# Differential queries and keys in 32-feature groups, gathered by transfers inside SBUF

## The chip, the core and the metric

One core of one Trainium2 chip runs the whole program. The metric is the device time in microseconds, the median of several runs; a profiled execution gives the trace beside it. Engines are named as the profile names them: PE (matmul), PEld (its weight loads), DVE (VectorE), ACT (ScalarE), POOL (GpSimd), SP (the queue that issues nearly all transfers).

## What is computed

A layer with two kinds of heads on 512 frames of width 2048: retention on one half, differential attention on the other, then an output projection and a gated projection. The part that the change touches is this (h heads of 2 × 64 features; `dv` are the values):

```python
u = rmsnorm(h, attn_norm[i])
z = u @ w_in[i]
...
dq = rmsnorm(dq.reshape(b, s, DIFF_HEADS, 2, DIFF_DH), diff_qn[i])
dk = rmsnorm(dk.reshape(b, s, DIFF_HEADS, 2, DIFF_DH), diff_kn[i])
...
sc = jnp.einsum('bqhcd,bkhcd->bhcqk', q_blk, kf)
pr = jax.nn.softmax(jnp.where(mask, sc, -jnp.inf), axis=-1)
attn = pr[:, :, 0] - lam * pr[:, :, 1]
out = jnp.einsum('bhqk,bkhe->bqhe', attn, vf)
```

The mask is causal in chunks of 64 frames, so a block of 128 queries sees 128, 256, 384 or 512 keys. Each of the 16 head components (8 heads × 2) is normed over its 64 features.

## The kernel before

Every float32 product is made of three matmuls on a high and a low part (`split`, `mm3`, L134 to L146): high times high, high times low, low times high. Features stand on the partitions, the 512 frames along the free dimension.

**Projections.** A chunk is 256 columns of a weight matrix. `wchunk` (L149) loads four blocks of 128 rows (512 KB) into the tile `raw` with the tag `wraw`, of which there are two buffers, and splits them into `wh` (ACT, L137) and `wl` (DVE, L138), of which there are four each. `wide_chunk` (L163) does the same for 512 columns at once. `proj_fm` (L225) accumulates a chunk in two of the four PSUM banks with the tag `acc`, `proj_wide` (L245) in all four. A load waits until the splits have read the buffer that it overwrites; a split waits until PE is done with the `wh` and `wl` four places before. Transfers and splits are given a high priority (`AHEAD`), so they stand as early in their queues as buffers allow. Each engine's queue, SP's among them, runs strictly in its order.

**Order of the work.** `run` advances a projection generator; at each yield `tick` counts up and runs what `agenda` holds for that tick. A tick is 12 matmuls of 512 columns. A projection of 256 columns has 8 ticks, a wide one 16. `after(n, f)` puts f at n ticks from now. A scheduler then lays out each engine's queue.

**Differential heads** go in four pairs (`pair_jobs`, L529): chunk `dq`, chunk `dk`, then other projections (`dg`, the wide `dv`), beside which the pair's steps are done. Here a chunk's two accumulators hold one head each: partitions 0 to 63 the first component, 64 to 127 the second. `qk_done` (L536) multiplies each accumulator with the row norm R1 (L541, frees the bank), then for each of the two heads makes a sum of squares (`squares`, L320: square, high, low), two matmuls against the block matrix `bd` (L347, L349), a chain of Ln, Exp, Square and three DVE operations (`rsqrt`, `normed`), and `stack_q` or `stack_k`, which write the operands in halves of 64 partitions: `qa` holds high over low of a component's queries, `k0` its keys' high part twice, `kz` their low part over zeros. The two norms are due at ticks `QK` after the chunk. `scores` (L475) makes, for each component, two matmuls into a bank of the tag `sc` (two banks), masks (L486), takes the maximum (L487) and the exponential with its sum (L488). `turn` transposes the probabilities, `values` multiplies with the values, `norm` ends a head. Their ticks are `SCORES`, `TURNS` and `VALUES`, counted from the end of `dk`.

Of the kernel before, what the change touches and what calls it, by code (L numbers as in the profile page):

```python
# [12 lines left out]
F32 = mybir.dt.float32  # L13
# [25 lines left out]
def f(ap):  # L39
    return ap.bitcast(F32)  # L40
# [3 lines left out]
def tile_layer(  # L44
# [42 lines left out]
    ct = const.tile([P, 43], F32, name="ct")  # L87
# [36 lines left out]
    g_dk = ct[:, 41:42]  # L124
# [4 lines left out]
    g_dq = const.tile([P, 1], F32, name="g_dq")  # L129
    nc.vector.tensor_scalar(g_dq, ct[:, 40:41], 0.125, None, ALU.mult)  # L130
    g_sub = const.tile([P, 1], F32, name="g_sub")
    nc.vector.tensor_scalar(g_sub, ct[:, 42:43], 0.8, None, ALU.mult)
# [16 lines left out]
    def wchunk(wd, n0, nk, name):  # L149
        wv = wd.rearrange("(kb p) n -> p kb n", p=P)  # L150
        for k0 in range(0, nk, 4):
            kn = min(4, nk - k0)
            with tc.high_priority(offset=AHEAD):
                raw = wpool.tile([P, 4, CW], F32, tag="wraw", name=f"wr_{name}_{k0}", bufs=2)
                nc.sync.dma_start(raw[:, :kn, :], wv[:, k0:k0 + kn, n0:n0 + CW])
# [164 lines left out]
    def squares(src, eps, name, pool=tmp):  # L320
        sq = pool.tile([P, S], F32, tag="sq", name=f"sq_{name}", bufs=2)
        nc.scalar.activation(sq, src, AF.Square)
        sh = pool.tile([P, S], F32R, tag="hi", name=f"sqh_{name}", bufs=1)
        sl = pool.tile([P, S], F32R, tag="lo", name=f"sql_{name}", bufs=1)
        nc.scalar.activation(sh, sq, AF.Identity, bias=eps)
        nc.vector.scalar_tensor_tensor(sl, sq, eps, f(sh), ALU.add, ALU.subtract)
        return sq, sh, sl

    def squares2(src, eps2, name, pool):

        lo, hi = slice(0, 64), slice(64, P)
        sq = pool.tile([P, S], F32, tag="sq", name=f"sq_{name}", bufs=2)
# [8 lines left out]
        return sq, s2, None  # L341

    def normed(t, sq, sel, width, tag, name, cut=None):

        z, sh, sl = sq
        ss = bank(tag, 1, f"ss_{name}")
        nc.tensor.matmul(ss, lhsT=sel, rhs=sh, start=True, stop=sl is None)  # L347
        if sl is not None:
            nc.tensor.matmul(ss, lhsT=sel, rhs=sl, start=False, stop=True)  # L349
# [90 lines left out]
    with ExitStack() as st:  # L440
        dp = st.enter_context(tc.tile_pool(name="dp", bufs=2))

        kz = [[dp.tile([P, S], F32R, tag=f"kz{j}{i}", name=f"kz{j}{i}", bufs=1) for i in range(2)]
              for j in range(2)]
        for pair in kz:
            for i, oth in enumerate((A1, A0)):
                nc.vector.memset(f(pair[i])[oth], 0.0)

        def stack_q(t, h):
            qa = dp.tile([P, S], F32R, tag="qa", name=f"qa{h}")  # L450
            qb = dp.tile([P, S], F32R, tag="qb", name=f"qb{h}")
            nc.scalar.activation(qa[A0], t[A0], AF.Copy, scale=g_dq[A0])
            nc.scalar.activation(qb[A1], t[A1], AF.Copy, scale=g_dq[A1])
            nc.vector.scalar_tensor_tensor(qa[A1], t[A0], g_dq[A0], f(qa)[A0], ALU.mult, ALU.subtract)
            nc.vector.scalar_tensor_tensor(qb[A0], t[A1], g_dq[A1], f(qb)[A1], ALU.mult, ALU.subtract)
            return qa, qb

        def stack_k(t, h):
            k0 = dp.tile([P, S], F32R, tag="k0", name=f"k0{h}")
            k1 = dp.tile([P, S], F32R, tag="k1", name=f"k1{h}")  # L460
            z0, z1 = kz[h % 2]
            nc.scalar.activation(k0[A0], t[A0], AF.Copy, scale=g_dk[A0])
            nc.scalar.activation(k1[A1], t[A1], AF.Copy, scale=g_dk[A1])
            nc.vector.tensor_copy(k0[A1], f(k0)[A0])
            nc.vector.tensor_copy(k1[A0], f(k1)[A1])
            nc.vector.scalar_tensor_tensor(z0[A0], t[A0], g_dk[A0], f(k0)[A0], ALU.mult, ALU.subtract)
            nc.vector.scalar_tensor_tensor(z1[A1], t[A1], g_dk[A1], f(k1)[A1], ALU.mult, ALU.subtract)
            return k0, k1

        def diff_steps(h, pair):  # L470
# [4 lines left out]
            def scores(b):  # L475
                qa, qb = pair["q", j]
                k0, k1 = pair["k", j]
# [4 lines left out]
                for i, (qs, ks) in enumerate(((qa, k0), (qb, k1))):  # L482
# [28 lines left out]
            def values():  # L511
# [9 lines left out]
                own["sq"] = squares2(own["o"], eps_d, f"d{h}", dp)  # L521

            def norm():
                normed(own["o"], own["sq"], ones, P, ("tp", "o")[j], f"d{h}", cut=thr)
                nc.vector.scalar_tensor_tensor(on_d[h], own["o"], g_sub, on_d[h], ALU.mult, ALU.mult)
# [3 lines left out]
        def pair_jobs(hp):  # L529
            pair = {}  # L530

# [4 lines left out]
            def qk_done(which, stack):  # L536
# [76 lines left out]
    with ExitStack() as st:  # L613
# [20 lines left out]
        def ret_steps(h):  # L634
# [34 lines left out]
            def norm():  # L669
                normed(on_r[h], own["sq"], ones, P, "tp", f"r{h}")  # L670
# [254 lines left out]
```

## Time and profile before

| | |
|---|---|
| median of 3 runs | 1083.37 us (1083.04 to 1083.54) |
| the profiled execution's own time | 1083.01 us |
| its span, first to last instruction | 1081.2 us |
| PE busy | 1074.7 us, 99% |
| PE weight loads busy | 900.7 us, 83% |
| DVE busy | 652.9 us, 60% |
| ACT busy | 561.2 us, 52% |
| transfers | 111.15 MB, 103 GB/s over the span |

A matmul's own time in the trace (389 ns for 512 columns) runs from its start to the end of its pipeline, and the next one starts before it ends. What a matmul costs PE is therefore the distance between two starts. "Idle before" of a group is time in which the engine did nothing just before its instructions, with what ended the wait.

### The profile page before, as it was taken

Reading aid. Unit: us, or ns where it says so; the run is one execution under the profiler, and the core shown is the slowest. Engines: PE = TensorE matmul, PEld = TensorE weight load, DVE = VectorE, ACT = ScalarE, POOL = GpSimd, SP = SyncE. Lnnn points to the kernel's source line nnn. Section 1 sums busy time; section 2 is a strip of 40 time slices with the busy share of each in tenths; the row PEclk is TensorE's granted clock in tenths of the full one; section 3 lists DMA queues with packets and bytes.
Section 4 is the critical chain, followed back from the end, with each engine's and each line's share of the span. In section 5 each row is a group of like instructions: output and inputs, shape, how many; then the busy total and the mean of one; then the engine's idle time right before and its main releaser. Section 6 shows DMA issues by size and latency. Waiting matters only on the chain.

```text
span 1081.2 us, 13724 instructions
## 1 busy us (share of the span) xinstructions
PE 1074.7 (99%) x5090; PEld 900.7 (83%) x5090; DVE 652.9 (60%) x1211; ACT 561.2 (52%) x1044; POOL 4.9 (0%) x14
## 2 busy tenths in 40 slices
PE   9999999999999999999999999999999999999998
PEld 8888888888888888888888988888888888888887
DVE  8677658775968786577446866844334453334442
ACT  8477657565767755664436655743333343222330
POOL 0000000000000000000000000000000000000000
PEclk9999999999999999999999999999999999999999
DMA  9232322322232232243322332463333323333341
GB/s 318 62 95 80 96 79 79 96 81 78 79 98 72 66 98 79 79 136 92 102 87 91 97 100 75 155 200 96 97 98 98 98 88 121 124 117 114 120 136 40
DMA packets 100579, 111.15 MB, mean 103 GB/s; under 512 B 4384, under 2 KB 88992, under 8 KB 100512
## 3 DMA queue, kind: packets, MB, share of 16 engines
q1 hardware_dynamic: 97632, 105.40, 31.7%
q10 hardware_dynamic: 2880, 4.87, 1.3%
q8 instruction: 40, 0.66, 0.3%
q14 instruction: 27, 0.22, 0.1%
HBM read 106.06 MB, written 4.19 MB: 102 GB/s over the span
## 4 chain that ended last, share of the span: by engine, by line
PE 98%; DVE 1%; ACT 0%; DMA 0%; issue 0%; ACTq 0%
PE acc_pg L145 5%; PE acc_pg L144 5%; PE acc_pg L146 5%; PE acc_o L146 5%; PE acc_o L145 5%; PE acc_o L144 5%; PE acc_dv L144 3%; PE acc_dv L145 3%; PE acc_dv L146 3%; PE acc_dq L144 3%; PE acc_rg L144 3%; PE acc_dq L145 3%; PE acc_dg L144 3%; PE acc_dk L144 3%; PE acc_dg L146 3%; PE acc_dg L145 3%
## 5 line engine op out<-in xcount | busy, mean ns | idle before, releaser
L144 PE MATMUL acc_o<-mh,wh_o 128*128 128x512 f32 x256 | 99.6, 389 | 0.0
L145 PE MATMUL acc_o<-ml,wh_o 128*128 128x512 f32 x256 | 99.6, 389 | 0.0
L146 PE MATMUL acc_o<-mh,wl_o 128*128 128x512 f32 x256 | 99.6, 389 | 0.0
L137 ACT ACTIVATE wh_o<-wr_o 128x512 fp32r<-128x512 f32 x64 | 40.4, 631 | 113.4 <-PE acc_o L145 106.7
L138 DVE TENSOR_TENSOR wl_o<-wr_o,wh_o 128x512 fp32r<-128x512 f32 x64 | 44.2, 691 | 89.2 <-ACT wh_o L137 89.2
L137 ACT ACTIVATE wh_pg<-wr_pg 128x512 fp32r<-128x512 f32 x56 | 35.4, 632 | 102.1 <-PE acc_pg L145 88.5
L144 PE MATMUL acc_pg<-hh,wh_pg 128*128 128x512 f32 x224 | 87.1, 389 | 0.0
L145 PE MATMUL acc_pg<-hl,wh_pg 128*128 128x512 f32 x224 | 87.1, 389 | 0.0
L146 PE MATMUL acc_pg<-hh,wl_pg 128*128 128x512 f32 x224 | 87.1, 389 | 0.0
L138 DVE TENSOR_TENSOR wl_pg<-wr_pg,wh_pg 128x512 fp32r<-128x512 f32 x56 | 38.7, 690 | 69.4 <-ACT wh_pg L137 69.4
L145 PEld LDWEIGHTS acc_o<-ml,wh_o 128*128 128x128 f32 x256 | 48.1, 188 | 10.0
L144 PEld LDWEIGHTS acc_o<-mh,wh_o 128*128 128x128 f32 x256 | 48.1, 188 | 10.0
L146 PEld LDWEIGHTS acc_o<-mh,wl_o 128*128 128x128 f32 x256 | 48.1, 188 | 9.8
L144 PE MATMUL acc_dv<-wh_dv,uh 128*128 128x512 f32 x128 | 51.0, 398 | 0.0
L144 PE MATMUL acc_dg<-uh,wh_dg 128*128 128x512 f32 x128 | 50.8, 397 | 0.0
L144 PE MATMUL acc_dk<-uh,wh_dk 128*128 128x512 f32 x128 | 50.4, 394 | 0.0
L144 PE MATMUL acc_rg<-uh,wh_rg 128*128 128x512 f32 x128 | 50.4, 394 | 0.0
L145 PE MATMUL acc_dk<-ul,wh_dk 128*128 128x512 f32 x128 | 50.1, 391 | 0.0
L146 PE MATMUL acc_dg<-uh,wl_dg 128*128 128x512 f32 x128 | 50.1, 391 | 0.0
L146 PE MATMUL acc_dv<-wh_dv,ul 128*128 128x512 f32 x128 | 50.1, 391 | 0.0
L145 PE MATMUL acc_dg<-ul,wh_dg 128*128 128x512 f32 x128 | 50.0, 391 | 0.0
L145 PE MATMUL acc_dv<-wl_dv,uh 128*128 128x512 f32 x128 | 50.0, 391 | 0.0
(318 smaller groups left out, 2824.1 us busy)
## 6 DMA issues: line engine op xcount, KB each, us to landing
wr_o<-w_out SPq DMA_DIRECT2D x32, 512.0 KB, 3.4
wr_pg<-w_gate SPq DMA_DIRECT2D x32, 512.0 KB, 3.5
wr_dk<-w_in SPq DMA_DIRECT2D x16, 512.0 KB, 3.6
wr_dg<-w_in SPq DMA_DIRECT2D x16, 512.0 KB, 3.7
wr_rg<-w_in SPq DMA_DIRECT2D x16, 512.0 KB, 3.6
wr_dq<-w_in SPq DMA_DIRECT2D x12, 512.0 KB, 3.7
wr_rv<-w_in SPq DMA_DIRECT2D x12, 512.0 KB, 3.9
wr_dv<-w_in SPq DMA_DIRECT2D x8, 512.0 KB, 3.9
```

Of the source, the lines that this page charges most:

```text
L137: nc.scalar.activation(hi, src, AF.Copy)
L138: nc.vector.tensor_tensor(lo, src, f(hi), ALU.subtract)
L144: nc.tensor.matmul(out, lhsT=ah, rhs=bh, start=start, stop=False, skip_group_check=True)
L145: nc.tensor.matmul(out, lhsT=ah, rhs=bl, start=False, stop=False, skip_group_check=True)
L146: nc.tensor.matmul(out, lhsT=al, rhs=bh, start=False, stop=stop, skip_group_check=True)
```

## The change

The columns of `w_in` that make the differential queries and keys are reordered on the host, so that a chunk's accumulator e holds features 32e to 32e+31 of all four components of the pair, in four groups of 32 partitions. Both accumulators then share one sum of squares per component: the squares are added, split once, multiplied with a `bd` of four 32 × 32 blocks, and one chain gives the factor for both. Each accumulator is split once, high and low, over all 128 partitions. The operands of the scores, `qd` (high over high), `qz` (low over zeros) and `kk` (high over low), are tiles of [128, 4, 512] with one buffer, and are put together by `gather`: four transfers of 32 partitions × 512 columns (64 KB) from SBUF to SBUF, issued on SP. A query chunk makes 24 of them, a key chunk 16. The tag `wraw` gets three buffers, and the ticks of the steps are new.

```diff
-SCORES = ((7, 11, 15, 19), (9, 13, 17, 21))
-TURNS = ((10, 14, 18, 22), (12, 16, 20, 25))
-VALUES = (25, 29)
-QK = (4, 6)
+SCORES = ((10, 13, 17, 21), (11, 15, 19, 23))
+TURNS = ((13, 16, 20, 24), (14, 18, 22, 26))
+VALUES = (27, 30)
+QK = 4
...
-    nc.vector.memset(f(bd)[0:64, 0:64], 1.0)
-    nc.vector.memset(f(bd)[64:128, 64:128], 1.0)
+    for g in range(0, P, 32):
+        nc.vector.memset(f(bd)[g:g + 32, g:g + 32], 1.0)
...
-                raw = wpool.tile([P, 2, S], F32, tag="wraw", name=f"wr_{name}_{k0}", bufs=2)
+                raw = wpool.tile([P, 2, S], F32, tag="wraw", name=f"wr_{name}_{k0}", bufs=3)
...
+        qd, qz, kk = (dp.tile([P, 4, S], F32R, tag=t, name=t, bufs=1) for t in ("qd", "qz", "kk"))
+        nc.vector.memset(f(qz)[64:], 0.0)
+
+        def gather(tile, row, src):
+            for g in range(4):
+                nc.sync.dma_start(f(tile)[row:row + 32, g, :], src[32 * g:32 * g + 32])
...
-                    nc.tensor.matmul(sc, lhsT=qs[:, c], rhs=ks[:, :L], start=True, stop=False)
-                    nc.tensor.matmul(sc, lhsT=qs[:, c], rhs=kz[j][i][:, :L], start=False, stop=True)
+                    nc.tensor.matmul(sc, lhsT=qd[:, g, c], rhs=kk[:, g, :L], start=True, stop=False)
+                    nc.tensor.matmul(sc, lhsT=qz[:, g, c], rhs=kk[:, g, :L], start=False, stop=True)
...
-                    sqs = [squares(pre[0], eps1, f"{which}{hp}_0")]
...
+                    x, sq = ([tmp.tile([P, S], F32, tag=t, name=f"{t}_{which}{hp}_{e}") for e in range(2)]
+                             for t in ("t0", "sq"))
+                    for e in range(2):
+                        nc.vector.tensor_tensor(x[e], acc[e], R1, ALU.mult)
+                    for e in range(2):
+                        nc.scalar.activation(sq[e], x[e], AF.Square)
+                    z = sq[0]
+                    nc.vector.tensor_tensor(z, z, sq[1], ALU.add)
...
+                    nc.scalar.activation(sh, z, AF.Identity, bias=eps2)
+                    nc.vector.scalar_tensor_tensor(sl, z, eps2, f(sh), ALU.add, ALU.subtract)
+
+                    def step():
+                        ss = bank("o", 1, f"ss_{which}{hp}")
+                        nc.tensor.matmul(ss, lhsT=bd, rhs=sh, start=True, stop=False)
+                        nc.tensor.matmul(ss, lhsT=bd, rhs=sl, start=False, stop=True)
+                        y = tmp.tile([P, S], F32, tag="y", name=f"y_{which}{hp}", bufs=1)
+                        rsqrt(y, z, ss, 1.0 / 64)
+                        nc.vector.scalar_tensor_tensor(y, z, 1.5, y, ALU.add, ALU.mult)
+                        for e in range(2):
+                            nc.vector.tensor_tensor(x[e], x[e], y, ALU.mult)
+                            hi = tmp.tile([P, S], F32R, tag="sq", name=f"{which}h{hp}_{e}")
+                            lo = x[e].bitcast(F32R)
+                            split(hi, lo, x[e], gain[:, e:e + 1])
+                            if which == "q":
+                                gather(qd, 32 * e, f(hi))
+                                gather(qd, 64 + 32 * e, f(hi))
+                                gather(qz, 32 * e, x[e])
+                            else:
+                                gather(kk, 32 * e, f(hi))
+                                gather(kk, 64 + 32 * e, x[e])
+
+                    after(QK, step)
```

`x` has the tag `t0` and the high part the tag `sq`, each with two buffers that the next chunk's `x` and squares use again. Counted in ticks from the end of the third pair's `dk`, the fourth pair's query step falls at 20 (8 ticks of `dg2`, 8 of `dq3`, 4 of `QK`), and the third pair's last scores at 21 and 23: these four score products read `qd` and `qz` as gathered for the fourth pair.

In the queues below an instruction is named by line, tiles and shape; `wr` is a raw load, `wl` the low part of a weight, `t_q` and `t_k` are `x`, `qh` is a high part, `acc` an accumulator, `sc` a bank of scores.

SP's queue at the third stage of the second pair (the wide projection `dv`), before:

```order
L170 DMA wr_dv_2_1951<-w_in 128x2x512
L170 DMA wr_dv_4_2009<-w_in 128x2x512
L170 DMA wr_dv_6_2081<-w_in 128x2x512
L170 DMA wr_dv_8_2135<-w_in 128x2x512
L170 DMA wr_dv_10_2195<-w_in 128x2x512
```

and with the change:

```order
L170 DMA wr_dv_4_2025<-w_in 128x2x512
L439 DMA qd<-qh_0_1747 32x512 x8
L170 DMA wr_dv_6_2059<-w_in 128x2x512
L439 DMA qz<-t_q_0_1640 32x512 x4
L439 DMA qd<-qh_1_1763 32x512
L170 DMA wr_dv_8_2093<-w_in 128x2x512
L439 DMA qd<-qh_1_1763 32x512 x7
L439 DMA qz<-t_q_1_1641 32x512 x4
L170 DMA wr_dv_10_2167<-w_in 128x2x512
```

The 24 gathers of the second pair's queries now stand between the loads of the wide projection, 11 of them behind load 8.

DVE's queue at the same place, with the change (before, the second accumulator's product, then L541, stood directly behind the low part of weight 3):

```order
L138 TENSOR_TENSOR wl_dv_3_2010<-wr_dv_2_1958,wh_dv_3_2009 128x512
L510 TENSOR_TENSOR t_k_0_1896<-acc_dk_0_1653,R_185 128x512
L293 SCALAR_TENSOR_TENSOR sq_d_1838<-ss_d_1935,sq_d_1838 128x512
L342 SCALAR_TENSOR_TENSOR y_d_1937<-ss_d_1935,thr,y_d_1937 128x512
L343 TENSOR_TENSOR ot_1836<-ot_1836,y_d_1937 128x512
L344 SCALAR_TENSOR_TENSOR ot_1836<-sq_d_1838,ot_1836 128x512
L495 SCALAR_TENSOR_TENSOR ond_751<-ot_1836,g_sub,ond_751 128x512
L510 TENSOR_TENSOR t_k_1_1897<-acc_dk_1_1654,R_185 128x512
L514 TENSOR_TENSOR sq_k_0_1898<-sq_k_0_1898,sq_k_1_1899 128x512
```

The product that frees the second accumulator of `dk` now writes the buffer that the gathers of `t_q_1` read.

PE's queue in the wide projection beside the fourth pair, where the third pair's last scores are, with the change:

```order
L144 MATMUL acc_dv_2_3590<-wh_dv_2_3660,uh_261 128x512
L454 MATMUL sc_3_0_3457<-kk,qd 128x512
L145 MATMUL acc_dv_2_3590<-wl_dv_2_3661,uh_261 128x512
L146 MATMUL acc_dv_2_3590<-wh_dv_2_3660,ul_262 128x512
L454 MATMUL sc_3_1_3463<-kk,qd 128x512
L144 MATMUL acc_dv_2_3590<-wh_dv_3_3709,uh_290 128x512
L145 MATMUL acc_dv_2_3590<-wl_dv_3_3710,uh_290 128x512
L146 MATMUL acc_dv_2_3590<-wh_dv_3_3709,ul_291 128x512
L455 MATMUL sc_3_0_3457<-kk,qz 128x512
L455 MATMUL sc_3_1_3463<-kk,qz 128x512
L454 MATMUL sc_3_0_3517<-kk,qd 128x512
```

Before, the second head's scores stood 29 matmuls behind the first head's, beside `dk`; now they follow at once, in the two banks that the first head's fill.

## Rows read from the trace of the kernel before

**Rows 1.** The page: span, busy time of PE, its clock by slices (tenths).

```profile
span 1081.2 us, 13724 instructions
...
PE 1074.7 (99%) x5090; PEld 900.7 (83%) x5090; DVE 652.9 (60%) x1211; ACT 561.2 (52%) x1044; POOL 4.9 (0%) x14
...
PEclk9999999999999999999999999999999999999999
```

**Rows 2.** Waits of PE, whole span: engine, line, what for: us in total, times, longest.

```profile
PE warm L111 <- DVE wide L108: 1.5, 1, 1.5
PE acc_dv L144 <- ACT uh L140: 0.4, 1, 0.4
```

**Rows 3.** Busy time in stretches: length, then PE, PEld, DVE, ACT, POOL (instructions), clock, DMA.

```profile
700.00:800.00 100.00, 100.00 (x443) 82.84 (x442) 44.00 (x67) 35.24 (x58) 0.00 (x0) 1.00 0.42 133
```

**Rows 4.** Groups of PE, the norm's matmuls: count, us busy, mean ns of one.

```profile
L347 PE MATMUL ss_q<-sqh_q,bd 128*128 128x512 f32 x8 | 3.4, 428 | 0.0
...
L349 PE MATMUL ss_q<-sql_q,bd 128*128 128x512 f32 x8 | 3.2, 399 | 0.0
```

**Rows 5.** Timeline of PE in the second pair's wide projection: start us, us.

```profile
175.77 0.39 PE L146 MATMUL acc_dk<-uh,wl_dk 128*128 128x512 f32 x1
175.99 0.39 PE L144 MATMUL acc_dv<-wh_dv,uh 128*128 128x512 f32 x1
...
178.72 0.40 PE L347 MATMUL ss_d<-sqh_d,ones 128*128 128x512 f32 x1
```

**Rows 6.** Timeline of ACT and DVE there.

```profile
177.29 0.63 ACT L137 ACTIVATE wh_dv<-wr_dv 128x512 fp32r<-128x512 f32 x1
```

```profile
175.68 0.68 DVE L541 TENSOR_TENSOR t_k<-acc_dk,R 128x512 f32<-128x512 f32 x1
...
178.12 0.69 DVE L138 TENSOR_TENSOR wl_dv<-wr_dv,wh_dv 128x512 fp32r<-128x512 f32 x1
178.73 0.68 DVE L541 TENSOR_TENSOR t_k<-acc_dk,R 128x512 f32<-128x512 f32 x1
```

**Rows 7.** Timeline of SP there, the load behind the split of weight 3.

```profile
178.84 0.37 SPq L170 DMA_DIRECT2D wr_dv<-w_in  x1
```

**Rows 8.** Waits of SP's queue: line, what for: us in total, times, longest.

```profile
SPq L170 <- DVE wl_dv L138: 30.0, 5, 8.0
```

**Rows 9.** Timeline of SP at the start, where issues follow each other.

```profile
0.75 0.39 SPq L96 DMA_DIRECT2D xt<-xT  x1
1.19 0.42 SPq L99 DMA_DIRECT2D xt<-xT  x1
1.66 0.42 SPq L92 DMA_DIRECT2D raw<-w_in  x1
```

**Rows 10.** Transfers by line: count, KB each, median us from issue to landing.

```profile
wr_dv<-w_in SPq DMA_DIRECT2D x8, 512.0 KB, 3.9
...
wr_pp<-w_proj SPq DMA_DIRECT2D x8, 256.0 KB, 2.8
...
outT<-h SPq DMA_DIRECT2D x2, 128.0 KB, 1.7
```

**Rows 11.** Timelines of PE and SP in the fourth pair's wide projection.

```profile
352.82 0.39 PE L146 MATMUL acc_dk<-uh,wl_dk 128*128 128x512 f32 x1
353.05 0.39 PE L144 MATMUL od<-ath,vh_dv 128*128 128x512 f32 x1
```

```profile
355.57 0.88 SPq L173 DMA_DIRECT2D wr_dv<-w_in  x2
```

**Rows 12.** Groups of DVE and ACT, a score of 512 keys: count, us busy, mean ns.

```profile
L487 DVE TENSOR_REDUCE sts<-sc 128x1 f32<-128x512 f32 x16 | 10.4, 686 | 0.0
...
L486 DVE MEMSET sc<- 64x64 f32 x64 | 6.4, 112 | 7.9 <-PE sc L485 7.4
```

```profile
L488 ACT ACTIVATION_READ_ACCUMULATOR p<-sc,sts 128x1 f32 x64 | 12.5, 195 | 0.0
...
L488 ACT ACTIVATE p<-sc,sts 128x512 f32<-128x512 f32 x16 | 10.9, 684 | 11.9 <-DVE sts L487 11.9
```

More of the change, by code (lines that the diff above doesn't have):

```diff
@@ L340, in squares2, with normed @@
             s2[hi], sq[lo], eps2[lo], f(s2)[lo], ALU.add, ALU.subtract).ins
-        return sq, s2, None
-    def normed(t, sq, sel, width, tag, name, cut=None):
-        z, sh, sl = sq
+        return sq, s2
+    def normed(t, sq, width, tag, name, cut=None):
+        z, s2 = sq
         ss = bank(tag, 1, f"ss_{name}")
-        nc.tensor.matmul(ss, lhsT=sel, rhs=sh, start=True, stop=sl is None)
-        if sl is not None:
-            nc.tensor.matmul(ss, lhsT=sel, rhs=sl, start=False, stop=True)
+        nc.tensor.matmul(ss, lhsT=ones, rhs=s2, start=True, stop=True)
         y = tmp.tile([P, S], F32, tag="y", name=f"y_{name}", bufs=1)
@@ L441, in tile_layer, with diff_steps @@
         dp = st.enter_context(tc.tile_pool(name="dp", bufs=2))
[L443 to L470, printed above, removed]
+        qd, qz, kk = (dp.tile([P, 4, S], F32R, tag=t, name=t, bufs=1) for t in ("qd", "qz", "kk"))
[3 more added lines that the diff above has]
+                nc.sync.dma_start(f(tile)[row:row + 32, g, :], src[32 * g:32 * g + 32])
+        def diff_steps(h):
             own = {}
@@ L529, in pair_jobs @@
         def pair_jobs(hp):
-            pair = {}
             def v_done(acc):
@@ L534, in v_done, with qk_done @@
                 split_v(vals[hp], acc)
[L536 removed]
+            def qk_done(which, gain):
                 def done(acc):
[L538 to L551 removed]
+                    x, sq = ([tmp.tile([P, S], F32, tag=t, name=f"{t}_{which}{hp}_{e}") for e in range(2)]
[6 more added lines that the diff above has]
+                    nc.vector.tensor_tensor(z, z, sq[1], ALU.add)
+                    sh, sl = (tmp.tile([P, S], F32R, tag=t, name=f"sq{t}_{which}{hp}", bufs=1)
+                              for t in ("hi", "lo"))
+                    nc.scalar.activation(sh, z, AF.Identity, bias=eps2)
[20 more added lines that the diff above has]
+                    after(QK, step)
@@ L556, in queue_heads @@
             def queue_heads():
-                late = 1 if hp == 3 else 0
-                last = (28, 34) if hp < 3 else (28, 32)
-                for j, (s, t, v, n) in enumerate((diff_steps(2 * hp + j, pair) for j in range(2))):
+                values, last = (VALUES, (30, 34)) if hp < 3 else ((27, 29), (30, 32))
+                for j, (s, t, v, n) in enumerate(diff_steps(2 * hp + j) for j in range(2)):
                     for b in range(4):
-                        after(late + SCORES[j][b], partial(s, b))
-                        after(late + TURNS[j][b], partial(t, b))
-                    after(VALUES[j], v)
+                        after(SCORES[j][b], partial(s, b))
+                        after(TURNS[j][b], partial(t, b))
+                    after(values[j], v)
                     after(last[j], n)
-            return v_done, qk_done("q", stack_q), qk_done("k", stack_k)
+            return v_done, qk_done("q", g_dq), qk_done("k", g_dk)
         vals = {}
@@ L858, in tile_layer @@
         for k0 in range(0, KB, 4):
-            raw = wpool.tile([P, 4, CW], F32, tag="wraw", name=f"wr_pg7_{k0}", bufs=2)
+            raw = wpool.tile([P, 4, CW], F32, tag="wraw", name=f"wr_pg7_{k0}", bufs=3)
             nc.sync.dma_start(raw, wv[:, k0:k0 + 4, 7 * CW:8 * CW])
@@ L898, in blocks, with halves @@
         return v.reshape(-1, P).T
-    def twice(v):
-        return np.concatenate([v, v]).reshape(P, 1)
+    def halves(v):
+        return np.tile(v.reshape(2, 1, 32), (1, 4, 1)).reshape(2, P).T
+    w_in = a["w_in"][0].copy()
+    for off in (OFF_DQ, OFF_DK):
+        w = w_in[:, off:off + 1024]
+        w[...] = w.reshape(D, 4, 4, 2, 32).transpose(0, 1, 3, 2, 4).reshape(D, 1024)
     cols = np.concatenate(
         [blocks(a["attn_norm"][0]), blocks(a["ple_norm"][0]), blocks(a["ret_gn"][0]),
-         twice(a["diff_qn"][0]), twice(a["diff_kn"][0]), a["diff_subln"][0].reshape(P, 1)], 1)
+         halves(a["diff_qn"][0]), halves(a["diff_kn"][0]), a["diff_subln"][0].reshape(P, 1)], 1)
     lams = np.stack([a["diff_lq1"][0], a["diff_lk1"][0], a["diff_lq2"][0], a["diff_lk2"][0]])
```

50 lines of the change are left out of this document (15 added, 35 removed).

## The prediction

> **What bounds the kernel now.** I read the page first: PE is busy for 1074.7 of 1081.2 us, at full clock (2.4 GHz) in every slice [rows 1]. The waits of PE come next, and they are the main finding: it waits twice, 1.9 us in all, both before its first real matmul [rows 2]. From then on nothing on DVE, ACT or SP is late for PE anywhere. The time is the number of matmuls times the distance between their starts, plus a start and a tail. That distance is not the 389 to 428 ns of a group row [rows 4], since matmuls overlap: 443 of them fill 100 us in the output projection [rows 3], 0.226 us each, and in the differential stage 12 starts take from 175.99 to 178.72 [rows 5], 0.2275 us each. So a change can gain only by taking matmuls away, and anything that comes late for PE is paid in full.
>
> **What the change removes.** The sums of squares of queries take two matmuls for each of 8 heads [rows 4], those of keys as many: 32. One pair of matmuls per chunk is left, 16 go. At 0.23 us that is -3.7 us. Bounds: -3.6 by [rows 3], and -6.6 if each cost its own duration (8 × 0.428 and 8 × 0.399 us, for queries and keys alike, halved); the starts speak for the first. Scores, transposes and values keep their matmuls: 0.
>
> For a chunk of queries DVE goes from 14 operations to 10 and ACT from 14 to 8, for keys DVE from 18 to 10. All of that is worth nothing by itself, since PE waits for none of it [rows 2]. A third `raw` buffer lets a load start earlier; no load is late, so 0. The `bd` memsets, two columns more in a constant and weights reordered on the host: 0, off PE's path.
>
> **What it adds.** 160 gathers of 64 KB on SP. Issues follow each other by 0.44 to 0.47 us [rows 9], 0.46 × 160 = 74 us of SP's queue spread over four pairs, and PE uses up a load of 512 KB in 24 matmuls, 5.5 us, which leaves SP time for both. By the difference of 512 and 256 KB, 3.9 - 2.8 us [rows 10], 64 KB occupy the transfer engines for 0.28 us: 45 us in total, beside engines that are busy 42% even in the stretch of [rows 3]. Neither is a price as such. The price is order. SP waits for the split of an older weight before most loads, 30 us in five waits in one wide projection [rows 8], and now gathers stand behind these waits; and ACT and DVE stand still where they would overwrite `x` or a high part that a gather still reads.
>
> *Second pair, wide projection.* The fourth accumulator takes the bank of `dk`'s second one, which L510 frees, and L510 writes the buffer of `t_q_1`: it waits until the last four `qz` gathers have landed. They are the last of 11 gathers behind load 8, and load 8 waits for the low part of weight 3. In the trace the load behind that split starts at 178.84 [rows 7], after 178.12 + 0.69 [rows 6]. The earliest would be the last `dk` matmul's end, 175.77 + 0.39 [rows 5], plus 0.63 and 0.69 us for the two splits [rows 6]: 177.48. From the load's issue: 11 × 0.46 = 5.1 us to the last gather, its landing, and 0.68 us for the product. No transfer inside SBUF is in the trace; the rows nearest in size go from 1.7 us (128 KB) to 3.9 us (512 KB) [rows 10]. I take 2.0, near the smaller, as a gather is half of it but often follows a load. So the bank is free 7.8 us after the issue, at 185.3 to 186.6. PE stands ready after 37 matmuls (three banks × four weights × 3, and one `ss_d`): 175.99 + 37 × 0.2275 = 184.4. The wait is 0.9 to 2.2 us; I take **1.7**, near the trace's own issue. With a landing of 1.7 or 3.9 us the ends are 0.6 and 4.1. Before, the product came at 178.73 [rows 6], long ahead.
>
> *Fourth pair, wide projection.* Here the third accumulator waits for `dk`'s first product, which waits for the `qz` gathers of `t_q_0`: five gathers behind load 8, which takes two issues. In the trace the corresponding load starts at 355.57 [rows 11]; the earliest is 352.82 + 0.39 + 0.63 + 0.69 = 354.53. The last of the gathers is issued 6 × 0.46 = 2.8 us later, lands 2.0 later, and the product takes 0.68: 360.0 to 361.0. PE is ready after 24 matmuls, 353.05 + 5.46 = 358.5 [rows 11]. The wait is 1.5 to 2.5; I take **2.0** (ends 1.2 and 4.4).
>
> *The third pair's last scores.* They need gathers nine issues further on, 358.3 + 9 × 0.46 + 2.0 = 364.4, where PE arrives 14 matmuls after the wait above, at 364.2: 0.2. Then the second head's scores follow at once, and their bank is free only after matmul, mask, maximum and exponential: 0.39 + 0.11 + 0.69 + 0.68 + 0.20 = 2.1 us [rows 12] less the two starts between, 0.46: 1.6. Together **1.8**; ends 0 (other work may fill it) and 2.5.
>
> *The other steps.* Scores and transposes of the two heads now start one tick apart (12 × 0.2275 = 2.7 us) where they were two apart, beside ACT and DVE that come out of such standstills. Four pairs with two such places each, at the 0.3 us by which one score chain of 2.1 us and one more DVE operation pass a tick: **2.4**; ends 0, as today, and 5.
>
> **Sum.** -3.7 + 1.7 + 2.0 + 1.8 + 2.4 = +4.2 us. The profiled execution took 1083.01 us, 1.8 more than its span: 1087.2. The median stands 0.36 above it: **1087.6 us**, slower by 0.4%. The ends of all terms are -4.8 and +12.4: 1078.6 and 1095.8; not all lie at one end together. A measurement of this kernel can tell about 0.2%, 2.2 us, from no change.
>
> **Rivals.**
>
> *The waits are covered, faster (0.11).* If a gather is issued in 0.26 us, its order costs 11 × 0.2 = 2.2 us less in the second pair and that wait is gone; the fourth pair's falls to 0.8, the scores' partly with it. About -3.7 + 1.0: 1080.7. The point is an issue of 0.26 us with all other steps free. For it: a gather has 32 rows where the transfers of [rows 9] have 128. Against it: a load of 512 rows takes 0.37 us [rows 7] and those 0.39 to 0.42, so the rows don't set it.
>
> *Half of the waits, no change (0.15).* Gathers that land in 1.0 us take 1.0 from each wide projection, and if half of the other steps stay covered the sum is +1.0: 1084.4. For it: 64 KB is half of the smallest row. Against it: a gather behind a load of 512 KB shares its engines. The Trainium skill ("DMA: Bandwidth & Descriptors", "Latency and other measured facts") says that the round trip to HBM is most of a transfer's fixed cost of about 2 us; a gather makes none, and by that rule this case is the likelier. No row here has such a transfer.
>
> *Gathers drain slowly, much slower (0.12).* A gather reads and writes 32 of 128 partitions. If its rate falls to a quarter, it takes 4 × 0.28 = 1.1 us and each waits for the one before: 11 × 0.64 = 7.0 us more in the second pair, 5 × 0.64 = 3.2 in the fourth: 1097.8. The Trainium skill ("SBUF — State Buffer", "Door 1: The DMA port swizzle") gives 32 partitions half of the ports; by that a gather would take 0.55 us, and 11 × 0.09 makes 1.0 us more, 1088.6. Nothing in this trace shows a transfer of 32 rows.
>
> **The numbers.** The forecast has 0.62. Slower by over 0.2%: the forecast and the slow drain, 0.74. Within 0.2%: 0.15. Faster: 0.11. The range reaches from the covered case to the slow drain, 1080 to 1098; the forecast's own is 1085 to 1093.
>
> **What would show it.** 16 PE instructions fewer (5074). Waits of PE at the fourth `acc_dv` bank of the second pair and the third of the fourth pair, ended by DVE, of 1 to 3 us each; in the same places DVE and ACT idle for 3 us or more, ended by transfers. Scores of 512 keys near 360 us that wait for ACT. Everything from 480 us on as before, shifted. PE without new waits would prove me wrong, and so would waits spread thinly over all score steps, or a loss in the starts of matmuls rather than in waits.

## The result, and the profile after

The changed kernel takes **1098.72 us** (median of 4 runs, 1098.4 to 1100.26), the kernel before 1083.30 us in the same comparison: a ratio of 1.0141, 95% interval 1.0128 to 1.0153, slower by 15.4 us. I had forecast 1087.6 us and a range up to 1098.

The page of the changed kernel, its span, its engines and the median time to landing (us) of the first kind of gathers, answers to [rows 1]:

```profile
span 1096.8 us, 13888 instructions
...
PE 1078.2 (98%) x5074; PEld 895.1 (82%) x5074; DVE 621.9 (57%) x1162; ACT 529.5 (48%) x996; POOL 4.9 (0%) x14
...
qd<-qh SPq DMA_DIRECT2D x64, 64.0 KB, 2.2
```

PE has its 16 instructions fewer, DVE and ACT are less busy by 31 and 32 us, and the span is longer by 15.6. Idle time alone doesn't say why: PE's busy time rose by 3.5 us although it does less. Two things happened, and the waits of PE show the first (engine, line, what for: us, times, longest), where [rows 2] had only the warm-up and `uh`:

```profile
PE acc_dv L144 <- DVE t_k L510: 5.7, 2, 3.5
PE warm L111 <- DVE wide L108: 1.5, 1, 1.5
PE sc L454 <- ACT p L458: 1.4, 2, 1.2
PE ss_d L338 <- DVE sqh_d L330: 1.1, 2, 0.6
PE rs L635 <- DVE ks L703: 0.9, 1, 0.9
PE sc L455 <- DMA qz<-t_q: 0.7, 1, 0.7
PE acc_dv L144 <- ACT uh L140: 0.5, 1, 0.5
```

*Second pair, wide projection.* The timeline of PE (start us, us, then in brackets the idle time before and what ended it) answers to [rows 5]:

```profile
184.88 0.39 PE L146 MATMUL acc_dv<-wh_dv,ul 128*128 128x512 f32 x1
188.76 0.79 PE L144 MATMUL acc_dv<-wh_dv,uh 128*128 128x512 f32 x1 [3.49 <-DVE t_k L510]
189.35 0.63 PE L145 MATMUL acc_dv<-wl_dv,uh 128*128 128x512 f32 x1
189.78 0.63 PE L146 MATMUL acc_dv<-wh_dv,ul 128*128 128x512 f32 x1
...
192.24 0.40 PE L146 MATMUL acc_dv<-wh_dv,ul 128*128 128x512 f32 x1
192.48 0.39 PE L522 MATMUL ss_k<-sqhi_k,bd 128*128 128x512 f32 x1
```

PE would have gone on at 185.11 and goes on at 188.76: 3.65 us. Then the second thing: the next matmuls start 0.43 us apart, not 0.2275. From 184.88 to 192.48 there are 10 starts, 2.3 us at the usual distance, in 7.6 us: **5.3 us** lost, 1.7 of them after the wait was over. The windows of that stretch (length, busy us of PE, PEld, DVE, ACT, POOL, then the granted clock) show why:

```profile
186.00:188.00 2.00, 0.00 (x0) 0.00 (x0) 0.00 (x0) 0.00 (x0) 0.00 (x0) 1.00 0.37 87
188.00:190.00 2.00, 1.24 (x3) 1.05 (x4) 1.29 (x2) 0.63 (x1) 0.00 (x0) 0.68 0.00 0
190.00:192.00 2.00, 2.00 (x6) 1.51 (x6) 1.21 (x3) 1.52 (x3) 0.00 (x0) 0.50 0.00 0
192.00:194.00 2.00, 2.00 (x10) 1.66 (x9) 1.59 (x3) 1.65 (x4) 0.00 (x0) 0.97 0.00 0
```

After the standstill the granted clock is 0.50, the lower level (1.2 GHz), for some 3 us. In the 40 slices of the page this can't be seen. SP and then DVE in the same place:

```profile
179.21 0.37 SPq L170 DMA_DIRECT2D wr_dv<-w_in  x1
179.62 4.35 SPq L439 DMA_DIRECT2D qd<-qh  x7
184.02 2.49 SPq L439 DMA_DIRECT2D qz<-t_q  x4
```

```profile
188.02 0.69 DVE L510 TENSOR_TENSOR t_k<-acc_dk,R 128x512 f32<-128x512 f32 x1 [2.23 <-DMA qz<-t_q]
```

The 11 gathers behind load 8 (issued at 179.21) are issued in 6.9 us, 0.63 each; the last lands at 187.9, and the product of L510 then frees the bank.

*Fourth pair, wide projection.* PE again, answering to [rows 11]:

```profile
361.01 0.39 PE L146 MATMUL acc_dv<-wh_dv,ul 128*128 128x512 f32 x1
363.57 0.50 PE L144 MATMUL acc_dv<-wh_dv,uh 128*128 128x512 f32 x1 [2.17 <-DVE t_k L510]
...
365.89 0.47 PE L454 MATMUL sc<-kk,qd 128*128 128x512 f32 x1 [0.44 <-DMA qd<-qh]
...
368.40 1.11 PE L455 MATMUL sc<-kk,qz 128*128 128x512 f32 x2 [0.65 <-DMA qz<-t_q]
370.69 0.50 PE L454 MATMUL sc<-kk,qd 128*128 128x512 f32 x1 [1.18 <-ACT p L458]
```

From 361.01 to 372.10 there are 21 starts, 4.8 us at the usual distance, in 11.1: **6.3 us** lost, first to L510, then to the third pair's last scores.

**The account.** Slower by 15.4 with 3.7 us of matmuls taken away makes 19.1 us lost: 5.3 and 6.3 in the two wide projections, and the remaining **7.5** in small pieces, from a few hundredths to 1.1 us, at scores, transposes and norms of all four pairs and at the first retention head (at 501.8 us). From 550 us on everything is shifted by the same 15.6.

Part of these pieces goes with the places of the scores in PE's queue, which are not those of the ticks. The first products of the first pair's first three score steps (the first block of each head, then the first head's second block), before:

```profile
92.23 0.22 PE L484 MATMUL sc<-k,qa 128*128 128x128 f32 x1
...
98.13 0.22 PE L484 MATMUL sc<-k,qa 128*128 128x128 f32 x1
...
104.15 0.28 PE L484 MATMUL sc<-k,qa 128*128 128x256 f32 x1
```

and with the change:

```profile
126.96 0.22 PE L454 MATMUL sc<-kk,qd 128*128 128x128 f32 x1
...
128.70 0.33 PE L454 MATMUL sc<-kk,qd 128*128 128x128 f32 x1 [0.21 <-ACT p L458]
...
131.19 0.36 PE L454 MATMUL sc<-kk,qd 128*128 128x256 f32 x1
```

By the ticks the first step would be 3 ticks (8 us) later than before, and the next two would follow by one and two ticks, 2.7 and 5.5 us. It is 35 us later, and they follow by 1.7 and 2.5 us: the scheduler, which lays out PE's queue, has put the steps far back and close together.

### The profile page after: what moved, and what is told of

Same layout as the page of the kernel before. It is cut to its first block, busy times and chain, and to the rows that moved or that the text cites. A ratio compares the mean times of both kernels' runs of the same rounds, so it can differ in the third digit from the quotient of the medians.

```text
span 1096.8 us, 13888 instructions
## 1 busy us (share of the span) xinstructions
PE 1078.2 (98%) x5074; PEld 895.1 (82%) x5074; DVE 621.9 (57%) x1162; ACT 529.5 (48%) x996; POOL 4.9 (0%) x14
## 4 chain that ended last, share of the span: by engine, by line
PE 55%; DVE 1%; ACT 0%; issue 0%; DVEq 0%
PE acc_pg L145 5%; PE acc_pg L146 5%; PE acc_pg L144 5%; PE acc_o L144 5%; PE acc_o L145 5%; PE acc_o L146 5%; PE acc_rg L144 3%; PE acc_rg L146 2%; PE acc_rg L145 2%; PE acc_rv L144 2%; PE acc_rv L146 2%; PE acc_rv L145 2%; PE acc_rk L146 1%; PE acc_rk L145 1%; PE acc_rk L144 1%; PE acc_rq L144 1%
## 5 line engine op out<-in xcount | busy, mean ns | idle before, releaser
L146 PE MATMUL acc_dk<-uh,wl_dk 128*128 128x512 f32 x128 | 50.2, 392 | 0.0
```

Of the source, the lines that this page charges most:

```text
L146: nc.tensor.matmul(out, lhsT=al, rhs=bh, start=False, stop=stop, skip_group_check=True)
```

## The experiments

The theory after this profile, "reused buffer": `x` has two buffers, L510 of the keys overwrites the queries' `x` while gathers read it, and so holds the bank that PE needs next. Rivals: gathers are late whatever buffer they read; SP's order; the third pair's late scores; closer ticks.

### The buffer, the order of the gathers, the late scores, and the clock

**x_own**

```diff
+                    xpool, xtag = (tmp, "t0") if which == "q" else (dp, "xk")
+                    x = [xpool.tile([P, S], F32, tag=xtag, ...) for e in range(2)]
...
-                raw = wpool.tile([P, 2, S], F32, tag="wraw", ..., bufs=3)
+                raw = wpool.tile([P, 2, S], F32, tag="wraw", ..., bufs=2)
```

> The changed kernel, with x of the keys in two buffers of its own (and two raw weight buffers instead of three, to make room). As in the changed kernel, four score products of the third pair read the fourth pair's queries. Theory 'reused buffer': PE's standstills in the wide projections (5.7 us at the accumulator banks that L510 frees, and 1.6 us of slow matmuls behind the longer one) come from L510 overwriting x while gathers read it; with buffers of its own both go, and the waits of the third pair's last scores with them in part: 1098.7 - 7.3 = 1091.4 us or a little less, and PE has no wait on L510. Rival 'the gathers themselves are late': the same gathers then hold up the scores that need them, waits of PE move from L510 to L454 and L455, and the time stays above 1096 us. Rival 'third raw buffer matters': with two of them PE waits for weight splits.

1087.94 us, ratio 1.0044 (1.0029 to 1.0058): 10.8 us less than the change, more than the 7.3 expected. PE's largest waits, and the windows of the two wide projections:

```profile
PE rs L636 <- DVE ks L704: 1.9, 1, 1.9
PE warm L111 <- DVE wide L108: 1.5, 1, 1.5
PE tr L475 <- DVE p L464: 1.2, 3, 0.5
```

```profile
174.00:194.00 20.00, 20.00 (x89) 16.26 (x88) 12.60 (x20) 11.49 (x20) 0.00 (x0) 1.00 0.56 154
350.00:374.00 24.00, 24.00 (x107) 19.39 (x106) 10.83 (x22) 9.66 (x19) 0.00 (x0) 1.00 0.45 132
```

No wait for the product, none for gathers or weights, and PE is busy and at full clock through both wide projections: nearly all of their 11.6 us is gone. Two raw buffers are enough. The theory holds; the rival falls. The third pair's last scores are no longer late either, but they also stand 25 to 56 places later in PE's queue than in the change and further apart, so this run doesn't say whether they were late because the bank was. The wait at the first retention head (`rs`) grew from 0.9 to 1.9 us.

**qz_first**

```diff
+                                gather(qz, 32 * e, x[e])
                                 gather(qd, 32 * e, f(hi))
                                 gather(qd, 64 + 32 * e, f(hi))
-                                gather(qz, 32 * e, x[e])
```

> The changed kernel with the order of a query chunk's gathers turned round: those that read x (qz) come ahead of the eight that read the high part (qd). As in the changed kernel, four score products of the third pair read the fourth pair's queries. 'Reused buffer': x is free eight issues, 8 x 0.635 = 5.1 us, earlier, more than the 3.5 and 2.2 us that PE waits for L510, so these waits and the slow matmuls behind them go without any memory: about 1091 us, while ACT's squares of the keys (L512) now wait for the high parts. Rival 'ACT is next': these squares stand in front of weight splits on ACT, PE then waits for high parts of weights, and the time is 1095 us or more. Rival 'gathers are late anyhow': 1097 to 1100 us.

1089.09 us, 1.0051 (1.0036 to 1.0066): 9.6 us come back from the order of three lines, without any memory. PE still waits 1.6 us for L510, in two places.

**scores19**

```diff
+                    early = ((10, 13, 16, 18), (11, 15, 17, 19))[j] if hp == 2 else SCORES[j]
                     for b in range(4):
-                        after(SCORES[j][b], partial(s, b))
+                        after(early[b], partial(s, b))
```

> The changed kernel with the third pair's scores at ticks 10, 13, 16, 18 and 11, 15, 17, 19, so all of them ahead of the fourth pair's gathers at tick 20; every score product then reads the queries of its own pair. Theory 'late scores': the 3.5 us that PE loses from 365 to 372 us (two waits for gathers, one for ACT) come from scores that wait for the next pair's gathers; without them 1098.7 - 3.5 = 1095.2 us. Rival 'one wait for another': the fourth pair's gathers write the tiles that these scores read, so they start later and x comes free later; the wait for L510 in the wide projection, 2.2 us there, grows by as much: 1097 to 1100 us.

1098.26 us, 1.0133 (1.0118 to 1.0148), no gain. Its waits:

```profile
PE acc_dv L144 <- DVE t_k L510: 6.4, 3, 3.5
PE ss_d L338 <- DVE sqh_d L330: 2.6, 3, 1.5
```

The scores no longer wait for gathers; beside the fourth pair, L510 and a norm now wait 4.5 us where L510 and the scores had waited 4.4: one wait took the other's place. That is not the whole of it. PE ran at a granted clock of 0.50 twice in this execution, behind idle times of 3.45 and 2.80 us, and lost 4.2 us by it against 1.7 in the profile of the change; beside the clock it lost 3.0 us less in all. In this run, in ticks and in the last four runs below, every score uses its own pair's queries; in the change and the other runs built on it, the third pair's last four score products use the fourth pair's.

**stalls**

```diff
+            nc.vector.tensor_copy(t[:, :8], src[:, :8])
+            for _ in range(n):
+                nc.vector.tensor_copy(t[:, :8], t[:, :8])
...
+                for a in acc:
+                    nc.vector.tensor_copy(a[:, :8], held_by[0][:, :8])
```

> The kernel before, with PE held between the column chunks of the output projection, seven times, by a chain of DVE copies of 8 columns that stands between the last matmul of a chunk and the first of the next: about 1, 1.8, 2.5, 3.2, 3.9, 4.8 and 5.2 us by the durations of the DVE operations in between. The output is the reference's. Theory 'clock': the granted clock falls to half after the longer of these standstills, as behind the 3.5 us in the changed kernel, and the next matmuls start 0.43 us apart instead of 0.23 for some 3 us, which costs 1.6 us each time on top of the wait; behind the shortest it does not. Rival 'no clock': matmuls behind every standstill start 0.23 us apart, and the slow ones in the changed kernel had another cause.

1113.69 us, in a single execution. PE's timeline, the first matmul behind four of the seven standstills, and the windows of the 2 us behind them:

```profile
776.15 0.47 PE L144 MATMUL acc_o<-mh,wh_o 128*128 128x512 f32 x1 [2.43 <-DVE acc_o L240]
...
802.90 0.47 PE L144 MATMUL acc_o<-mh,wh_o 128*128 128x512 f32 x1 [3.10 <-DVE acc_o L240]
...
828.78 0.77 PE L144 MATMUL acc_o<-mh,wh_o 128*128 128x512 f32 x1 [3.84 <-DVE acc_o L240]
...
886.69 0.76 PE L144 MATMUL acc_o<-mh,wh_o 128*128 128x512 f32 x1 [5.13 <-DVE acc_o L240]
```

```profile
776.10:778.10 2.00, 1.95 (x7) 1.61 (x8) 1.82 (x3) 0.32 (x1) 0.00 (x0) 0.76 0.82 261
802.90:804.90 2.00, 2.00 (x9) 1.65 (x10) 1.18 (x2) 0.00 (x0) 0.00 (x0) 1.00 0.60 209
828.80:830.80 2.00, 2.00 (x5) 1.63 (x6) 0.50 (x1) 0.00 (x0) 0.00 (x0) 0.50 0.24 79
856.90:858.90 2.00, 1.99 (x5) 1.61 (x6) 0.00 (x0) 0.00 (x0) 0.00 (x0) 0.50 0.00 0
886.70:888.70 2.00, 2.00 (x5) 1.61 (x6) 0.00 (x0) 0.00 (x0) 0.00 (x0) 0.50 0.00 0
```

The clock theory holds: behind 3.84, 4.72 and 5.13 us of idle PE ran at 0.50, and the matmuls that followed lost 1.5, 2.7 and 1.6 us against their usual distance. It is no simple step, though: 2.43 us cost 1.7 us (a few matmuls later), 3.10 nothing, 1.02 and 1.70 nothing. Nor is a short standstill safe: in the run poolq below PE stood idle for 1.56 us at 360.1, the clock fell 1 us after it went on, and 1.7 us were lost.

### The rest: ticks, queue, and the matmuls taken away

**ticks**, on top of x_own

```diff
+                    near = hp == 2
+                    sc = (((10, 14, 18, 22), (12, 16, 20, 24)), ((10, 13, 16, 18), (11, 15, 17, 19)))[near][j]
+                    tu = (((13, 17, 21, 25), (15, 19, 23, 26)), TURNS)[near][j]
```

> The kernel with x of the keys in buffers of its own (1087.9 us), with the two heads' scores two ticks apart again (10, 14, 18, 22 and 12, 16, 20, 24, transposes three ticks on); the third pair's scores all ahead of the fourth pair's gathers, so every score reads its own pair's queries. What that kernel still loses against the kernel before, 8.5 us in the starts of PE, is spread over scores, transposes and norms between 100 and 510 us. Theory 'closer ticks': about half of it comes from the two heads' steps standing one tick apart; with two ticks 1083.5 to 1086 us. Rival 'not the ticks': the steps have become late themselves, as gathers come between the norm and the scores; the time stays at 1087 to 1089 us.

1085.94 us, 1.0029 (1.0019 to 1.0039): 2.0 us of the 8.5 by the medians, with intervals that overlap, just inside the range of the first theory. The run says little on closer ticks, though. All but the last two of the first pair's 16 scores stand in PE's queue where x_own has them, so the new ticks hardly moved them. About 1.5 of the 2.0 us come at the first retention head, where PE waits 0.4 us and not 1.9. What the closeness of the steps costs stays open.

**x_qz** (x_own and qz_first in one)

> Both remedies for x: buffers of its own for the keys' x, and the gathers that read x ahead of those that read the high part. As in the changed kernel, four score products of the third pair read the fourth pair's queries. If both only take away the same wait for L510, they don't add: 1087 to 1089 us. If gathers late for other steps still cost something, the second gives a part of it back: under 1086.5 us.

1088.16 us, 1.0046 (1.0031 to 1.0061). They remove the same wait and don't add. (In the profiled execution, 1088.93 us, the clock was at 0.50 once more, from 493.0 us on, behind 2.2 us of idle.)

**poolq**

```diff
-                nc.sync.dma_start(f(tile)[row:row + 32, g, :], src[32 * g:32 * g + 32])
+                nc.gpsimd.dma_start(f(tile)[row:row + 32, g, :], src[32 * g:32 * g + 32])
```

> The changed kernel with its 160 gathers issued on POOL, which has nothing else to do, instead of SP. As in the changed kernel, four score products of the third pair read the fourth pair's queries. Theory 'SP's order': gathers wait behind loads whose raw buffer isn't free, and for their turn of 0.635 us behind one another; on a queue of their own they start as soon as the split is done, x comes free earlier, and the time is 1087 to 1092 us. Rival 'a gather's own issue': if POOL takes longer than 0.635 us for each, a chunk's 24 gathers take longer than the 15 us they take now, x comes free later, and the time is over 1099 us.

1088.83 us, 1.0056 (1.0041 to 1.0071). POOL takes 0.50 us for a gather, and PE waits 1.0 us for L510. The window behind PE's idle time of 1.56 us:

```profile
363.00:365.00 2.00, 2.00 (x6) 1.61 (x5) 1.74 (x5) 0.84 (x3) 0.00 (x0) 0.50 0.00 0
```

With **prio**, on SP but ahead of loads, the same comes out:

```diff
+            with tc.high_priority(offset=2 * AHEAD):
                 for g in range(4):
```

> The changed kernel with the gathers given a higher priority than loads, so that they stand in SP's queue ahead of loads that are not yet due. As in the changed kernel, four score products of the third pair read the fourth pair's queries. Theory 'SP's order': gathers no longer stand behind loads that wait for a split, x comes free earlier and PE's waits for L510 shrink from 5.7 to under 2.5 us: 1089 to 1093 us. Rival 'loads become late': 16 to 24 gathers at 0.635 us, 10 to 15 us, stand ahead of loads that PE needs every 5.5 us; PE waits for weights, and the time is above 1096 us.

1088.36 us, 1.0046 (1.0032 to 1.0060), with 3.0 us of waits for the same product (there L511). In its transfers all four kinds of gathers land in the same time:

```profile
qd<-qh SPq DMA_DIRECT2D x64, 64.0 KB, 2.0
...
kk<-t_k SPq DMA_DIRECT2D x32, 64.0 KB, 2.0
```

So four edits that share nothing but an earlier end of the `x` gathers, or no need of it, each give back about 10 us.

**no_low**, on the kernel before

```diff
-        if sl is not None:
-            nc.tensor.matmul(ss, lhsT=sel, rhs=sl, start=False, stop=True)
```

> The kernel before without the second matmul, that of the low part, in the sums of squares of queries and keys: 16 matmuls fewer, as in the change, and nothing else of the change. The sum of squares so loses its low part. By the distance of starts, 16 x 0.23 = 3.7 us: 1079.4 us. By the matmuls' own durations 6.6 us: 1076.5 us. If PE had slack there: 1083 us.

1083.52 us, 1.0003 (0.9993 to 1.0012): **nothing**, the outcome to which I gave least thought. PE waits where it never had:

```profile
PE sc L483 <- DVE kz L465: 2.0, 3, 0.8
...
PE sc L482 <- ACT p L486: 1.3, 2, 0.6
```

The waits lie among the first scores of each pair: PE has four matmuls fewer to do there and comes 0.9 us sooner to operands that are ready when they were. **no_low_t1** moves scores and transposes one tick on:

```diff
-                late = 1 if hp == 3 else 0
+                late = 1
```

> The kernel before without the second matmul of the sums of squares of queries and keys (their low part is left out, 16 matmuls fewer), and with scores and transposes of all four pairs one tick later, as the fourth pair's were already. Without the tick those 16 matmuls gave nothing: PE then waited for the operands at the first scores of each pair, 3.3 us in all, and 0.3 in small ones. Theory 'no wait was not slack': the scores stood just behind their operands, so that PE now only arrives earlier; one tick later, 12 x 0.2275 = 2.7 us, the waits go and 16 x 0.23 = 3.7 us are gained: 1079.6 us. Rival 'DVE and ACT bound the pair': the waits turn up further on, at transposes, values or norms, and the time stays at 1083 us.

1081.75 us, 0.9987 (0.9977 to 0.9996): 1.6 of the 3.7 us. In PE's queue the first scores of three pairs are indeed 12 places later, one tick, and the waits for `kz` are gone there. The one that is left, 0.8 us, is the fourth pair's, whose ticks the edit doesn't change. So the slack was about zero; the rest is thin at scores and transposes.

### What the gathers themselves cost, and a version to beat both

**no_gather**, on top of ticks

```diff
-            for g in range(4):
-                nc.sync.dma_start(f(tile)[row:row + 32, g, :], src[32 * g:32 * g + 32])
+            pass
```

> The kernel of the run with two ticks between the heads' scores (1085.9 us), without any gather: the operands of the scores are zeros, all else is computed as there. Theory 'gathers': what that kernel still loses against the kernel before, 6.7 us, is the lateness of gathers and of what they hold up; without them 1079.5 to 1081 us. Rival 'order of the work': the loss comes from where scores, transposes and norms now stand among the projections; without gathers the time stays at 1084 to 1086 us.

1080.38 us, 0.9975 (0.9966 to 0.9985): 5.5 us under ticks, where PE waits for no reused `x` (ACT's squares of the keys still wait for gathers, 2.0 us in four), and 3.0 of the 3.7 us are gained. But taking the gathers away changed more than the transfers. The first pair's first two score steps here:

```profile
99.48 0.22 PE L454 MATMUL sc<-kk,qd 128*128 128x128 f32 x1
...
105.38 0.22 PE L454 MATMUL sc<-kk,qd 128*128 128x128 f32 x1
```

In ticks they start at 124.7 and 126.4. Without gathers the scheduler puts the steps near their ticks again, some 6 us apart, and against the usual distance of starts PE loses nothing at scores, where it lost 3.2 us in ticks. So 5.5 us is the price of the gathers together with the order that the scheduler makes around them; the rival 'order of the work' is not parted from the gathers by this run.

**best1**, on top of x_own and qz_first, with the ticks of the run ticks for the first three pairs

```diff
+                          ((10, 13, 16, 19), (11, 15, 18, 21)))[max(hp - 1, 0)][j]
...
+                          ((13, 16, 19, 22), (14, 18, 21, 24)))[max(hp - 1, 0)][j]
...
+                    after(values[j] if hp < 3 else (25, 28)[j], v)
+                    after(last[j] if hp < 3 else (28, 31)[j], n)
```

> A version that may beat both: x of the keys in buffers of its own, gathers that read x first, two ticks between the heads' scores in the first two pairs, the third pair's scores ahead of the fourth pair's gathers, and the fourth pair's scores, values and norms one to two ticks earlier than in the change, so that the retention heads behind them start on time. Every score reads its own pair's queries. If the waits at the end of the differential stage (norms, retention's first scores and splits, 2.3 us in the run with two ticks) go, 1083 to 1084 us; if also those at the second and third pairs' first transposes, 1080 to 1082 us; if the fourth pair's steps now come too early for their operands, 1086 us or more.

1084.31 us, 1.0008 (0.9998 to 1.0017), level with the kernel before. The losses at the end of the differential stage are gone (PE's starts from 450 to 525 us are on time but for 0.3 us); those at scores stay. Three more runs asked why.

**best2** (`QK = 3`), **best6** (`QK = 3`, and the first scores a tick later) and **best4** (`QK = 3`, and the key gathers ahead of loads):

```diff
+                                with tc.high_priority(offset=2 * AHEAD):
                                     gather(kk, 32 * e, f(hi))
                                     gather(kk, 64 + 32 * e, x[e])
```

> The version that came level with the kernel before (1084.3 us), with the norm step of queries and keys at tick 3 instead of 4: the gathers start one tick, 2.7 us, earlier against the scores. Theory 'gathers late for scores': what is left, 4.8 us in the starts of PE against the kernel before, lies at scores that wait for the last gathers of the keys; with 2.7 us more they find them: 1080.5 to 1082.5 us. Rival 'the norm is late too': the step waits for its own squares on ACT and DVE, nothing starts earlier: 1084 us or more.

> The norm step at tick 3 and, in the first, second and fourth pairs, the first scores of each head one tick later (11 and 13, and 11 and 12): two ticks, 5.5 us, more between the norm and the scores than in the version that came level. If the scores only wait for gathers, 1080 to 1081.5 us, near the 1080.4 us of the kernel without gathers; if one tick was enough, the same as the run with the norm step at tick 3 alone; if something else is late, no gain over 1084.3 us.

> As the run before it, with the norm step at tick 3, and the key gathers of each pair ahead of loads in SP's queue (queries' gathers stay as they are). Theory 'gathers late for scores': 1080 to 1082 us, and key gathers land in about 2.0 us instead of 3.0 to 3.3. Rival 'loads become late': 16 gathers at 0.635 us, 10 us, stand ahead of loads and PE waits for weights: 1085 us or more.

best2: 1084.29 us, 1.0009 (1.0000 to 1.0018). best6: 1084.65 us, 1.0012 (1.0003 to 1.0021). best4: 1082.65 us, 0.9996 (0.9988 to 1.0005). In best6 the scores of the first two pairs, a tick later in the agenda, stand in PE's queue exactly where best1 and best2 have them: there the ticks don't set the order, the scheduler does. So neither run says what 2.7 us more would do. Putting the key gathers ahead of loads moves the scores forward; median landings of key gathers, best2 and then best4:

```profile
kk<-t_k SPq DMA_DIRECT2D x32, 64.0 KB, 3.3
```

```profile
kk<-t_k SPq DMA_DIRECT2D x32, 64.0 KB, 2.0
```

It gains 1.6 us by the medians, less than expected and with intervals that overlap, and is level with the kernel before, not faster. Why many score steps with gathers start a few hundredths to a tenth of a us late, while the trace names no wait, stays open; that it goes away without gathers is shown by no_gather alone, which also changes the order.

## Why the prediction was wrong

The direction, the two places, the releaser and the chain were right: PE waits at the fourth accumulator of the second pair and the third of the fourth pair, ended by L510, which was ended by `qz` gathers; DVE idled 5.6 and ACT 7.1 us there; the 512-key scores near 360 us waited for ACT. The sizes were off, by 11 us; even all upper ends together, +12.4, fall short of +15.4. Term by term:

- **Second pair, 1.7 us; 5.3 came.** The step "11 × 0.46" failed: I took the issue time from [rows 9], transfers of 128 rows, and a gather takes 0.58 to 0.60 us of SP and 0.63 from start to start, 11 × 0.17 = 1.9 us more. That is about the whole difference of the wait itself (3.65). The landing of 2.0 us and the 0.68 us of the product were right (185.9 + 2.0, then 188.02). I even wrote that "the rows don't set it", of a transfer's issue, and priced only an issue faster than 0.46 as a rival, none slower.
- **The missing term: the clock, 1.7 us.** Nothing in the trace of before shows PE standing still after its start, and [rows 1] has full clock in every slice, so I paid a wait once. This wait was paid one and a half times. I named "a loss in the starts of matmuls" as what would prove me wrong; here it was part of the loss.
- **Fourth pair and third pair's last scores, 2.0 + 1.8; 6.3 came.** The wait for L510 was 2.2 us as forecast; the load (357.21 against 354.5 to 355.6) and PE (361.24 against 358.5) were both later than I had them. The scores were the error: nine issues at 0.63 instead of 0.46, and two waits for gathers, not one. The runs add that the parts aren't additive as I had them: with the scores moved away L510 and a norm waited longer (scores19).
- **Other steps, 2.4 us, bound 5; 7.5 came.** The step "Four pairs with two such places each, at the 0.3 us" took the steps to stand one tick apart, 2.7 us. In PE's queue they don't: with gathers in the program the first ones start 1.7 and 2.5 us apart. The 0.3 doesn't follow from its rows either, as 2.1 + 0.69 passes 2.73 by less than 0.1. And I had set the gathers at "Neither is a price as such"; no_gather shows 5.5 us for them and the order that they bring. How the two share it stays open.
- **Matmuls taken away, -3.7 us.** The account closes with it, and no_gather comes to -3.0. But the reason given, that anything saved on PE is gained because PE waits for nothing, is false: no_low took the same number away and gained nothing. A trace without waits can still have no slack.
- **0 for fewer DVE and ACT operations, the third raw buffer and `bd`**: nothing speaks against it; x_own does without the third buffer and PE waits for no weight.

The upper end, 1098, was the slow drain, which comes close in time but was not what happened: gathers are paced by SP's issue, not by their drain. In prio they follow each other by 0.63 us and land in 2.0 all the same, so none waits for the one before. The Trainium skill ("SBUF — State Buffer", "Door 1: The DMA port swizzle") gives 32 partitions half of the ports, which made my estimate of 0.55 us for a gather; as the issue is longer, no run here tells that from 0.28.

The rival "half of the waits" rested on a landing of 1.0 us. A gather alone lands in 2.0 us; the first five behind load 8 land in 4.2 to 2.5. The Trainium skill ("DMA: Bandwidth & Descriptors", "Latency and other measured facts") puts most of a transfer's fixed cost of about 2 us down to the receipt round trip to the target memory, and has HBM as the slowest target. No saving by staying inside SBUF shows in these runs, since 128 KB to HBM land in 1.7 us [rows 10], and the measurement decides.

## What to carry to other kernels

A transfer between a producer and its consumer makes its source a buffer that stays in use until the landing: ask who writes it next, what that writer frees, and put first the transfers whose source is wanted back. Where no engine waits, don't take it for slack: count how far operands are ahead of their use before pricing a saving or a new latency. Look up in the queue where a scheduler has put each step, rather than in the agenda that it was given. And price a transfer's issue from one with the same shape, or bound it on the slow side too; 160 small transfers on one queue are 100 us of that queue.

## What was not expected of the hardware

- After idle times of 3.5 to 5.1 us of PE the granted clock stood at 0.50 for 3 us or more (1.5 to 2.7 us lost each time). After 1.02, 1.70 and 3.10 us (stalls) it didn't fall; after 1.56 (poolq), 2.16 (x_qz), 2.43 (stalls) and 2.80 us (scores19) it did, for a loss of 1.5 to 1.7 us. So the length of the standstill alone doesn't decide.
- Issuing a transfer of 32 partitions × 2 KB takes SP 0.58 to 0.60 us, longer than a load of 512 KB (0.37 us); POOL takes 0.50.
- Such a transfer inside SBUF lands in 2.0 us, no sooner than one of 128 KB to HBM.
